# The last quarter of an MLP by two seven-product units, the final norm's factors by pieces, a tile pool 32 bytes lower, and relu squares on ScalarE

## The chip, the cores and the metric

The kernel runs on one core of a Trainium2 chip. Its engines are TensorE (PE, with PEld for its weight loads), VectorE (DVE), ScalarE (ACT), GpSimd (POOL) and SyncE (SP), which issues most DMAs. Each engine works through its own instructions in order and waits on semaphores for the others. The metric is the device time of one execution in microseconds (us), as the median of the runs.

## The reference

One layer of a streaming encoder for 256 tokens of width 2048 and 256 memory tokens, all float32:

```python
h = rms_norm(x, norm_mix_g);  x = x + hybrid_mixer(h, ...)      # retention + gated delta rule
h = rms_norm(x, norm_x_g);    x = x + cross_attention(h, rms_norm(mem, norm_mem_g), w_xq, w_xkv, w_xo)
h = rms_norm(x, norm_ffn_g);  x = x + square(relu(h @ w_ff1)) @ w_ff2   # 2048 -> 8192 -> 2048
return rms_norm(x, norm_final_g)        # x * rsqrt(mean(x*x) + 1e-6) * g
```

Here `x` is 256 by 2048, `w_ff1` 2048 by 8192, `w_ff2` 8192 by 2048. The change touches the MLP, the final norm, and where the tiles for memory lie.

## The kernel before

Every large product keeps float32 precision by three matmuls on a faster type: each operand is split into a high part (a ScalarE copy, L125) and a low part (a VectorE subtraction, L126), and high·high, high·low and low·high are added up in PSUM. Activations lie in quads: tiles of four feature blocks of 128, high and low beside each other (`q` in the trace). Weights come by DMA in pieces of 1 MB into `raw` (three buffers), and `fetch` converts each piece in two halves of 128x1024 into `whi` and `wlo` (three buffers, and every fourth pair `whx`, `wlx` in the MLP). `fetch` runs with a priority far ahead of other work, so that DMAs and conversions run ahead as far as the buffers go.

The stages, by the span of the profiled execution: cross-attention's values of the memory tokens (to 97 us: L401 to L403 and, in `chunk`, L166 to L168, with memory's quads as the stationary operand), its keys (to 191 us: `blocks`, L210 and L211, with memory's quads as the moving operand of a 512 and a 256 column matmul), the mixer (to 1066 us), output projection and cross-attention (to 1372 us), and the MLP.

The MLP runs in four quarters (`fb`) of 2048 hidden units, which start at 1372, 1527, 1697 and 1867 us. Each quarter first makes its hidden units with `blocks(h3, w_ff1, ...)`, eight times two blocks of 128 (L210 and L211), evacuated in `evac_h`: `bo` is the sum of two parts of PSUM (L220, L221), `hs` its squared relu, and hs is split into the quarter's quads. Then `with_seven` multiplies them by the quarter's rows of `w_ff2`, for four groups of 512 columns (n) and two halves of the tokens (t), by four quarters of the rows (q). A plain product (`plain(n, q)`) is 24 matmuls of 512 columns. A unit of seven products does what eight would (Strassen's way, Winograd's form) for the row quarters 0 and 1 and a pair of column groups: sums of token halves (`token_sums`, tile `sv`, its split `sh`, `sl`) times sums of weight blocks (b11, b12, b22, b21, made in place in the tiles `rt` and `tr`). One product (`product`) is 12 matmuls; it first converts its block in two halves (L1205, L1206) and, where `then` is given, makes a weight sum (L1210). `read` puts finished PSUM results on a list, and the next product's `read_now` adds them to the residual `res` on VectorE (`add`, L1141), behind the conversions that are out by then. All matmuls of plain and seven-product work have L1185. On PE the order is the order in which the code issues them (`ends` keeps the blocks and the products in turn).

The quarters 1 and 2 (`early`) have two such units for 16, so 14 products and 8 plain ones. The quarters 0 and 3 have one unit and twelve plain ones. In quarter 3 the last group of 512 columns is done by `chunk` at the very end, with its token half 1 in two halves of 256 columns, 96 half-width matmuls, and `evac_last` adds, squares, and scales. The final norm's sums of squares of the first three groups are taken on ScalarE (`square_sum`), their products with the final gain on VectorE (L1365), the root on POOL (L267); then each row block of 128 tokens is scaled by its root and written out. The final gains are read into `gfin`, which is the buffer of b22.

The tile pools lie behind one another in SBUF. PAD1 sets the length of a padding tile in front of the pool that holds memory's quads: these start at 117760 bytes of a partition and 4096 bytes on (multiples of 64). The activation quads (from 68064 on), weight tiles and the quads at 130016 and on start 32 bytes beside a multiple of 64.

Of the kernel before, what the change touches and what calls it, by code (L numbers as in the profile page):

```python
# [10 lines left out]
F32 = mybir.dt.float32  # L11
# [6 lines left out]
P = 128  # L18
D = 2048
# [15 lines left out]
PAD1, PAD2 = 144, 80  # L35
# [17 lines left out]
def trunk(ctx: ExitStack, tc: tile.TileContext, x_f, mem_f, positions, lead_f, small_f, w_in, ret_gn_g, w_out, w_xq,  # L53
# [1081 lines left out]
    gfin = b22  # L1135
# [8 lines left out]
    def add_later(n, t, ps):  # L1144

        with tc.issue_after(latest["lo"]):
            add(n, t, ps)

# [10 lines left out]
    def with_seven(hid, rows, last, early):  # L1159
# [39 lines left out]
        def product(o, lhs, raw, key, then=None):  # L1199

            halves = []
# [10 lines left out]
            for i in range(4):  # L1212
                ins = triple(o, lhs(i), [a[:, i % 2, :] for a in halves[i // 2]], key, i == 3)
            ends.append(ins)
# [11 lines left out]
        if early:  # L1226
# [20 lines left out]
            load_block(b12, 0, 3)  # L1247
            product(own[1][0], summed(3), b22, (1, 0))
# [3 lines left out]
            read((0, 0, own[0][0]))  # L1252
            product(own[0][1], part(1, 1), b11, (0, 1))
            read((0, 1, own[0][1]))
# [9 lines left out]
            read(*((1, t, own[1][t]) for t in range(NT)))  # L1264
# [9 lines left out]
            read(*((3, t, own[3][t]) for t in range(NT)))  # L1274
            product(own[2][0], part(1, 0), b21, (2, 0))
            read((2, 0, own[2][0]))
            product(shared, summed(2), b12, "shared")
            read((2, 1, shared), (3, 1, shared))
            product(own[2][1], part(1, 1), b11, (2, 1))
            read((2, 1, own[2][1]))  # L1280
        else:
# [3 lines left out]
            first = 2 if last else 3  # L1285
            plain(first, 0)
            load_block(b11, 0, 0)
            plain(first, 1)
# [3 lines left out]
            plain(first, 2)  # L1292
# [5 lines left out]
            plain(first, 3)  # L1298
            load_block(b21, 1, 0)
            read(*((first, t, own[first][t]) for t in range(NT)))  # L1300
# [5 lines left out]
            if not last:  # L1306
                plain(2, 0)
# [3 lines left out]
            if not last:  # L1311
                plain(2, 1)
            product(own[0][1], part(1, 1), b11, (0, 1))
            read((0, 1, own[0][1]))
            if not last:
                plain(2, 2)
                plain(2, 3)
                read(*((2, t, own[2][t]) for t in range(NT)))
            plain(1, 3)
            read(*((1, t, own[1][t]) for t in range(NT)))  # L1320
        for those in reads:
            add(*those)

    ends = []
    for fb in range(4):
        hid = []
        rows = w_ff2[0, fb * D:(fb + 1) * D, :]
        early = fb in (1, 2)
        parts_of = with_seven(hid, rows, fb == 3, early)
        ends.clear()  # L1330
        for b2 in range(8):
# [4 lines left out]
            def evac_h(b, ps):  # L1336
                if early and b2 > 3:
                    act.activation(ps, ps, AF.Relu)
                    act.activation(hs[:, b, :], ps, AF.Square)
                else:  # L1340
                    vec.scalar_tensor_tensor(hs[:, b, :], ps, 0.0, ps, op0=ALU.max, op1=ALU.mult)
# [13 lines left out]
        if fb < 3:  # L1355
            continue
        with tc.issue_after(fetched[-1]):
            nc.sync.dma_start(gfin, norm_final_g.partition_broadcast(P))
        for t in range(NT):
            for n in range(3):  # L1360
                ns = slice(n * 512, (n + 1) * 512)
                got = res[:, t, ns]
                square_sum(ssq4[:, t, n:n + 1], got)
                with tc.issue_after(latest["add"]):
                    vec.tensor_mul(got, got, gfin[:, ns])  # L1365
        for n in range(3, 4):
            ns = slice(n * 512, (n + 1) * 512)

            def evac_last(t, ps, c0, c1):
                got = add(n, t, ps, c0, c1)  # L1370
                acc = ssq4[:, t, 4 if c0 else 3:5 if c0 else 4]
                if t == 0:
                    square_sum(acc, got)
                else:
                    junk = sm.tile([P, 512], F32, name="junk", tag="junk", bufs=1)
                    vec.scalar_tensor_tensor(junk[:, :256], got, 1.0, got, op0=ALU.mult, op1=ALU.mult, accum_out=acc)
                if not c0:
                    s = sm.tile([P, 1], F32, name="s4", tag="s4")
                    vec.tensor_reduce(s, ssq4[:, t, 0:4], axis=AX.X, op=ALU.add)
                    vec.tensor_scalar(s, s, 1.0 / D, EPS, op0=ALU.mult, op1=ALU.add)  # L1380
                    sums.append(s)
                else:
                    vec.scalar_tensor_tensor(sums[t], acc, 1.0 / D, sums[t], op0=ALU.mult, op1=ALU.add)
                if c1 < 512:
                    return
                r = sm.tile([P, 1], F32, name="r4", tag="r4")
                rsqrt(r, sums[t])
                if t == 0:
                    vec.tensor_mul(res[:, t, ns], res[:, t, ns], gfin[:, ns])
                for c in (0, 3, 1, 2):  # L1390
                    cs = slice(c * 512, (c + 1) * 512)
                    o = res[:, t, cs]
                    if t and c == 3:
                        vec.scalar_tensor_tensor(o, o, r, gfin[:, cs], op0=ALU.mult, op1=ALU.mult)
                    elif t and c == 2:
                        vec.tensor_scalar(o, o, r, None, op0=ALU.mult)
                    else:
                        act.activation(o, o, AF.Copy, scale=r)
                    (act if t and c in (3, 2) else nc.sync).dma_start(out[0, t * P:(t + 1) * P, cs], o)

            sums = []
# [43 lines left out]
```

## Time and profile before

| | |
|---|---|
| median of 3 runs | 2051.8 us (2050.77 to 2052.64) |
| profiled execution | 2050.97 us, span 2049.2 us |
| granted clock of TensorE | 0.999 |
| PE, DVE, ACT, POOL busy | 99%, 75%, 56%, 2% |
| DMA | 405.24 MB, mean 198 GB/s |
| last quarter of the MLP | from 1867 us: blocks to 1956, second matrix to 2041, then norm and output |

The profile's span begins with the first instruction that it shows, and the execution has 1.77 us more around it. In the views a row is an instruction (start, length, engine, line, operation, output and inputs by tile) or a group of them. PE's ends are modelled, so its pace is read from one start to the next.

### The profile page before, as it was taken

How to read it: one execution, taken by the hardware profiler on the slowest of the kernel's cores; microseconds unless marked ns; L12 is line 12 of the kernel's file. 1: busy time of each engine (PE TensorE's matmuls, PEld its weight loads, DVE VectorE, ACT ScalarE, POOL GpSimd, SP SyncE). 2: the span in 40 equal slices, each digit the busy share in tenths (PEclk: the TensorE clock that was granted, in tenths of full speed). 3: DMA queues.
4: the chain of work that ended last, by engine and by line, in shares of the span. 5: the costliest groups of instructions: out<-in, count | busy, mean ns of one | idle time of the engine just before them, and what ended most of it. 6: DMA issues, size and time to landing. Idle time of an engine off the chain costs nothing.

```text
span 2049.2 us, 28493 instructions
## 1 busy us (share of the span) xinstructions
PE 2038.1 (99%) x10850; PEld 1756.6 (86%) x10850; DVE 1542.9 (75%) x2433; ACT 1153.2 (56%) x1871; POOL 36.3 (2%) x50
## 2 busy tenths in 40 slices
PE   9999999999999999999999999999999999999998
PEld 8888888988888888888888899888888888888887
DVE  5887788779667875888557666777868887888785
ACT  6655764575457555755446555555545655655554
POOL 0000000000000000000000000000000000000000
PEclk9999999999999999999999999999999999999999
DMA  9679556555555555555467655569657647555662
GB/s 327 204 253 301 185 183 196 164 185 195 187 168 181 194 196 165 184 182 189 156 206 248 191 180 163 173 180 257 219 169 234 219 159 218 200 199 159 220 217 103
DMA packets 329225, 405.24 MB, mean 198 GB/s; under 512 B 34928, under 2 KB 239360, under 8 KB 328960
## 3 DMA queue, kind: packets, MB, share of 16 engines
q1 hardware_dynamic: 328656, 402.74, 61.1%
q8 instruction: 85, 1.39, 0.3%
q10 hardware_dynamic: 432, 0.69, 0.1%
q14 instruction: 52, 0.43, 0.1%
HBM read 389.74 MB, written 11.55 MB: 196 GB/s over the span
## 4 chain that ended last, share of the span: by engine, by line
PE 96%; DMA 1%; DVE 1%; issue 1%; ACT 1%; SPq 0%; POOLq 0%; POOL 0%; DVEq 0%; ACTq 0%
PE s L210 33%; PE s L211 17%; PE s L167 8%; PE s L168 8%; PE s L166 8%; PE b L1185 7%; PE s L1185 6%; PE s L401 1%; PE s L403 1%; PE s L402 1%; PE b L796 1%; PE b L829 1%; PE b L138 0%; DMA raw<-w_ff 0%; PE b L137 0%
## 5 line engine op out<-in xcount | busy, mean ns | idle before, releaser
L210 PE MATMUL s<-q,whi 128*128 128x512 f32 x2816 | 972.6, 391 | 0.8 <-DVE bo L221 0.6
L126 DVE TENSOR_TENSOR wlo<-raw,whi 128x1024 fp32r<-128x1024 f32 x592 | 722.6, 1222 | 294.9 <-ACT whi L125 288.5
L125 ACT ACTIVATE whi<-raw 128x1024 fp32r<-128x1024 f32 x592 | 627.4, 1060 | 518.9 <-PE s L210 189.2
L211 PE MATMUL s<-q,wlo 128*128 128x256 f32 x2816 | 769.3, 280 | 0.7 <-DVE wlo L126 0.6
L210 PEld LDWEIGHTS s<-q,whi 128*128 128x128 f32 x2816 | 520.8, 188 | 102.9 <-DVE bo L221 0.9
L211 PEld LDWEIGHTS s<-q,wlo 128*128 128x128 f32 x2816 | 528.6, 188 | 13.1 <-DVE wlo L126 1.6
L167 PE MATMUL s<-wlo,q 128*128 128x512 f32 x716 | 281.6, 393 | 0.0
L168 PE MATMUL s<-whi,q 128*128 128x512 f32 x716 | 279.3, 390 | 0.0
L166 PE MATMUL s<-whi,q 128*128 128x512 f32 x716 | 258.9, 390 | 0.0
L166 PEld LDWEIGHTS s<-whi,q 128*128 128x128 f32 x716 | 134.3, 188 | 27.9
L168 PEld LDWEIGHTS s<-whi,q 128*128 128x128 f32 x716 | 134.6, 188 | 26.9
L167 PEld LDWEIGHTS s<-wlo,q 128*128 128x128 f32 x716 | 134.6, 188 | 26.7
L220 ACT ACTIVATE bo<-s 128x256 f32<-128x256 f32 x192 | 72.8, 379 | 107.2 <-PE s L211 107.1
L221 DVE TENSOR_TENSOR bo<-bo,s 128x256 f32<-128x256 f32 x192 | 79.9, 416 | 48.6 <-ACT bo L220 48.3
L125 ACT ACTIVATE whx<-raw 128x1024 fp32r<-128x1024 f32 x56 | 59.3, 1059 | 53.7 <-PE s L210 21.9
L210 PE MATMUL s<-q,whx 128*128 128x512 f32 x256 | 89.2, 389 | 0.0
L126 DVE TENSOR_TENSOR wlx<-raw,whx 128x1024 fp32r<-128x1024 f32 x56 | 68.4, 1221 | 24.6 <-ACT whx L125 24.1
L1185 PE MATMUL s<-whi,q 128*128 128x512 f32 x264 | 85.2, 389 | 0.0
L1185 PE MATMUL b<-whi,q 128*128 128x512 f32 x244 | 78.8, 389 | 0.0
L1206 DVE TENSOR_TENSOR wlo<-rt,whi 128x1024 fp32r<-128x1024 f32 x46 | 56.1, 1223 | 23.3 <-ACT whi L1205 22.5
L211 PE MATMUL s<-q,wlx 128*128 128x256 f32 x256 | 70.5, 280 | 0.0
L1205 ACT ACTIVATE whi<-rt 128x1024 fp32r<-128x1024 f32 x46 | 48.8, 1060 | 33.4 <-PE s L1185 15.3
(385 smaller groups left out, 2344.7 us busy)
## 6 DMA issues: line engine op xcount, KB each, us to landing
raw<-w_in SPq DMA_DIRECT2D x143, 1024.0 KB
raw<-w_ff SPq DMA_DIRECT2D x104, 1024.0 KB
raw<-w_xkv SPq DMA_DIRECT2D x29, 1024.0 KB
raw<-w_out SPq DMA_DIRECT2D x16, 1024.0 KB
raw<-w_xq SPq DMA_DIRECT2D x16, 1024.0 KB
raw<-w_xo SPq DMA_DIRECT2D x16, 1024.0 KB
rt<-w_ff SPq DMA_DIRECT2D x12, 1024.0 KB
tr<-w_ff SPq DMA_DIRECT2D x12, 1024.0 KB
```

Of the source, the lines that this page charges most:

```text
L125: latest["hi"] = act.activation(hi[:, cs], src[:, cs], AF.Copy).ins
L126: latest["lo"] = vec.tensor_sub(lo[:, cs], src[:, cs], hi[:, cs].bitcast(F32)).ins
L166: pe.matmul(o, xh, wh, start=first, stop=False)
L167: pe.matmul(o, xh, wl, start=False, stop=False)
L168: pe.matmul(o, xl, wh, start=False, stop=last)
L210: pe.matmul(ps[b], lh, xhl, start=kk == 0, stop=False)
L211: ins = pe.matmul(ps[b][:, :S], ll, xh, start=False, stop=kk == KT - 1).ins
L220: act.activation(o, ps[b][:, S:], AF.Copy)
L221: vec.tensor_add(o, o, ps[b][:, :S])
L1185: ins = pe.matmul(o, lhs[l], rhs[r], start=key not in opened, stop=last and j == 2, skip_group_check=True).ins
L1205: latest["hi"] = act.activation(hi, raw[:, c:c + 1024], AF.Copy).ins
L1206: latest["lo"] = vec.tensor_sub(lo, raw[:, c:c + 1024], hi.bitcast(F32)).ins
```

## The change

The change has four parts.

1. `PAD1` goes from 144 to 136 floats: all tiles of the pool behind it, memory's quads among them, start 32 bytes lower (117728).
2. `early` holds for quarter 3 too: it has 14 products and 8 plain ones. Its last product goes in two halves of 256 columns into two PSUM tiles, 24 half-width matmuls.
3. The final norm's factors come by pieces: as soon as a piece of `res` is complete, `settle` takes its squares on ScalarE and multiplies it by the final gain on VectorE, in the middle of the products. The gains have a quad buffer of their own and are fetched in the middle of the quarter. Row block 0's root and scaling are issued ahead of the last product's sums; row block 1's last piece is squared on VectorE, in two halves.
4. In the quarters 1 to 3 all of `evac_h`'s squared relus run on ScalarE (Relu in PSUM, then Square into `hs`); before, ScalarE had those of the last four of eight steps in the quarters 1 and 2, and VectorE had the others.

```diff
-PAD1, PAD2 = 144, 80
+PAD1, PAD2 = 136, 80
...
+    def settle(n, t):
+        got = res[:, t, n * 512:(n + 1) * 512]
+        square_sum(ssq4[:, t, (0, 1, 3, 2)[n]:(1, 2, 4, 3)[n]], got)
+        vec.tensor_mul(got, got, final[0][:, n * 512:(n + 1) * 512])
+
+    def mean_square(t):
+        s = sm.tile([P, 1], F32, name="s4", tag="s4")
+        vec.tensor_reduce(s, ssq4[:, t, 0:4], axis=AX.X, op=ALU.add)
+        vec.tensor_scalar(s, s, 1.0 / D, EPS, op0=ALU.mult, op1=ALU.add)
+        sums.append(s)
+
+    def finish_row(t):
+        r = sm.tile([P, 1], F32, name="r4", tag="r4")
+        rsqrt(r, sums[t])
+        for c in (0, 2, 1, 3):
+            cs = slice(c * 512, (c + 1) * 512)
+            o = res[:, t, cs]
+            if t and c == 2:
+                vec.scalar_tensor_tensor(o, o, r, final[0][:, cs], op0=ALU.mult, op1=ALU.mult)
+            elif t and c == 3:
+                vec.tensor_scalar(o, o, r, None, op0=ALU.mult)
+            else:
+                act.activation(o, o, AF.Copy, scale=r)
+            (act if t and c > 1 else nc.sync).dma_start(out[0, t * P:(t + 1) * P, cs], o)
...
         def read_now():
-            for those in reads:
-                add_later(*those)
+            for n, t, ps, *done in reads:
+                add_later(n, t, ps)
+                if last and done:
+                    settle(n, t)
...
             load_block(b12, 0, 3)
+            if last:
+                final.append(quad_a().both.rearrange("p k s -> p (k s)").bitcast(F32))
+                with tc.issue_after(fetched[-1]):
+                    nc.sync.dma_start(final[0], norm_final_g.partition_broadcast(P))
...
-            read((0, 0, own[0][0]))
+            read((0, 0, own[0][0], True))
...
             product(own[2][0], part(1, 0), b21, (2, 0))
-            read((2, 0, own[2][0]))
+            read((2, 0, own[2][0], True))
+            if last:
+                read((2, 1, own[2][1]))
             product(shared, summed(2), b12, "shared")
-            read((2, 1, shared), (3, 1, shared))
-            product(own[2][1], part(1, 1), b11, (2, 1))
-            read((2, 1, own[2][1]))
+            if last:
+                mean_square(0)
+                finish_row(0)
+            read((2, 1, shared), (3, 1, shared, True))
+            if not last:
+                product(own[2][1], part(1, 1), b11, (2, 1))
+                read((2, 1, own[2][1]))
+            else:
+                ends_of = stream_ps()
+                product(ends_of, part(1, 1), b11, "end")
+                for c, ps in enumerate(ends_of):
+                    got = add(2, 1, ps[:, :256], c * 256, c * 256 + 256)
+                    junk = sm.tile([P, 512], F32, name="junk", tag="junk", bufs=1)
+                    acc = ssq4[:, 1, 3 + c:4 + c]
+                    vec.scalar_tensor_tensor(junk[:, :256], got, 1.0, got, op0=ALU.mult, op1=ALU.mult, accum_out=acc)
+                    if c:
+                        vec.scalar_tensor_tensor(sums[1], acc, 1.0 / D, sums[1], op0=ALU.mult, op1=ALU.add)
+                    else:
+                        mean_square(1)
+                finish_row(1)
...
-        early = fb in (1, 2)
+        early = fb > 0
...
-                if early and b2 > 3:
+                if early:
                     act.activation(ps, ps, AF.Relu)
                     act.activation(hs[:, b, :], ps, AF.Square)
...
-            chunk(hid, cols(rows, n * 512), evac_last, hold=quad_b)
```

The instructions of all engines stand in the same order up to the MLP's quarter 1, where the squared relus move; PE's and the DMA queue's up to quarter 3.

First place: VectorE at the very end of the program. In the names, `res` is the residual, `s0`, `s1` and `b` are PSUM tiles, `junk` receives squares whose sum goes to `ssq4`, `tr` and (after) `q` hold the final gains, and L1153 is the new product by the gain. Before:

```order
L1141 SCALAR_TENSOR_TENSOR res_13006<-s0_18616,rstd3q_13000,res_13006 128x512
L1379 TENSOR_REDUCE s4_18754<-ssq4_13012 128x1
L1389 TENSOR_TENSOR res_13006<-res_13006,tr_13007 128x512
L1380 TENSOR_SCALAR s4_18754<-s4_18754 128x1
L1141 SCALAR_TENSOR_TENSOR res_13006<-s1_18617,rstd3q_13000,res_13006 128x256
L1376 SCALAR_TENSOR_TENSOR junk_18793,ssq4_13012<-res_13006 128x256
L1379 TENSOR_REDUCE s4_18795<-ssq4_13012 128x1
L1380 TENSOR_SCALAR s4_18795<-s4_18795 128x1
L1141 SCALAR_TENSOR_TENSOR res_13006<-b_18618,rstd3q_13000,res_13006 128x256
L1376 SCALAR_TENSOR_TENSOR junk_18823,ssq4_13012<-res_13006 128x256
L1383 SCALAR_TENSOR_TENSOR s4_18795<-ssq4_13012,s4_18795 128x1
```

And now, behind the last product's last conversion:

```order
L1153 TENSOR_TENSOR res_13006<-res_13006,q_18324 128x512
L1157 TENSOR_REDUCE s4_18789<-ssq4_13012 128x1
L1141 SCALAR_TENSOR_TENSOR res_13006<-b_17779,rstd3q_13000,res_13006 128x512 x2
L1158 TENSOR_SCALAR s4_18789<-s4_18789 128x1
L1141 SCALAR_TENSOR_TENSOR res_13006<-s0_18802,rstd3q_13000,res_13006 128x256
L1141 SCALAR_TENSOR_TENSOR res_13006<-s1_18803,rstd3q_13000,res_13006 128x256
L1153 TENSOR_TENSOR res_13006<-res_13006,q_18324 128x512
L1329 SCALAR_TENSOR_TENSOR junk_18842,ssq4_13012<-res_13006 128x256
L1157 TENSOR_REDUCE s4_18844<-ssq4_13012 128x1
L1329 SCALAR_TENSOR_TENSOR junk_18848,ssq4_13012<-res_13006 128x256
L1158 TENSOR_SCALAR s4_18844<-s4_18844 128x1
L1331 SCALAR_TENSOR_TENSOR s4_18844<-ssq4_13012,s4_18844 128x1
```

Before, the first half's square and sum stood ahead of the last add; now the product by the gain, both squares and the sum stand behind it.

Second place: VectorE in the middle of the last quarter's products, at the plain product of column group 3 and row quarter 2, whose conversions are the L126 of `raw_18648` (L1239 makes weight sums). Now:

```order
L126 TENSOR_TENSOR wlx_18595<-raw_18588,whx_18594 128x1024
L1235 TENSOR_TENSOR wlo_18627<-tr_13007,whi_18626 128x1024
L1141 SCALAR_TENSOR_TENSOR res_13006<-b_17780,rstd3q_13000,res_13006 128x512 x2
L1153 TENSOR_TENSOR res_13006<-res_13006,q_18324 128x512
L1235 TENSOR_TENSOR wlo_18631<-tr_13007,whi_18630 128x1024
L1239 TENSOR_TENSOR rt_10152<-tr_13007,rt_10152 128x1024 x2
L1153 TENSOR_TENSOR res_13006<-res_13006,q_18324 128x512
L126 TENSOR_TENSOR wlo_18651<-raw_18648,whi_18650 128x1024
L126 TENSOR_TENSOR wlx_18655<-raw_18648,whx_18654 128x1024
```

Before, the products by the gain stood behind the last of the products, among the last chunk's conversions:

```order
L126 TENSOR_TENSOR wlo_18684<-raw_18681,whi_18683 128x1024
L1141 SCALAR_TENSOR_TENSOR res_13006<-s0_18157,rstd3q_13000,res_13006 128x512
L1141 SCALAR_TENSOR_TENSOR res_13006<-s1_18158,rstd3q_13000,res_13006 128x512
L1365 TENSOR_TENSOR res_13006<-res_13006,tr_13007 128x512
L126 TENSOR_TENSOR wlx_18688<-raw_18681,whx_18687 128x1024
L1365 TENSOR_TENSOR res_13006<-res_13006,tr_13007 128x512 x5
```

Six products by the gain stood in one place with a single conversion behind the first; now they lie one by one among the conversions.

More of the change, by code (lines that the diff above doesn't have):

```diff
@@ L1263, in with_seven @@
             plain(1, 3)
-            read(*((1, t, own[1][t]) for t in range(NT)))
+            read(*((1, t, own[1][t], True) for t in range(NT)))
             product(p5, summed(0), b11, "p5", (b11, b22, b11))
@@ L1310, in with_seven @@
             read((0, 1, shared), (1, 1, shared))
-            if not last:
-                plain(2, 1)
+            plain(2, 1)
             product(own[0][1], part(1, 1), b11, (0, 1))
             read((0, 1, own[0][1]))
[L1315 to L1318, printed above, removed]
+            plain(2, 2)
+            plain(2, 3)
+            read(*((2, t, own[2][t]) for t in range(NT)))
             plain(1, 3)
             read(*((1, t, own[1][t]) for t in range(NT)))
-        for those in reads:
-            add(*those)
+        for n, t, ps, *_ in reads:
+            add(n, t, ps)
     ends = []
@@ L1354, in trunk @@
             pass
[L1355 to L1401, printed above, removed]
-            chunk(hid, cols(rows, n * 512), evac_last, hold=quad_b)
```

28 lines of the change are left out of this document (14 added, 14 removed).

## The prediction

> **What bounds the kernel now.** I read the page's busy shares first, then its chain of work that ended last:
>
> ```profile
> PE 2038.1 (99%) x10850; PEld 1756.6 (86%) x10850; DVE 1542.9 (75%) x2433; ACT 1153.2 (56%) x1871; POOL 36.3 (2%) x50
> PE 96%; DMA 1%; DVE 1%; issue 1%; ACT 1%; SPq 0%; POOLq 0%; POOL 0%; DVEq 0%; ACTq 0%
> ```
>
> TensorE (PE) is busy for 99% of the span and is 96% of the chain. So time goes only where there are fewer matmuls, where one takes less, where PE stops waiting, or in the tail behind the last matmul. The profiled execution took 2050.97 us, 0.83 below the median of 2051.8. I sum against 2050.97 and add 0.83 at the end. A measurement of this kernel can tell about 0.2% from no change, 4.1 us: faster means under 2047.7, slower over 2055.9.
>
> **Memory's quads, 32 bytes lower.** PE's timeline shows the pace of 512-column matmuls while those quads are the stationary operand (L401 to L403 and L167), and the chain a stretch of the MLP where the pace is that of other operands:
>
> ```profile
> 21.15 0.40 PE L401 MATMUL s<-whi,q 128*128 128x512 f32 x1
> ...
> 49.62 0.40 PE L403 MATMUL s<-whi,q 128*128 128x512 f32 x1
> ...
> 76.16 0.40 PE L167 MATMUL s<-wlo,q 128*128 128x512 f32 x1
> ...
> 90.16 0.40 PE L167 MATMUL s<-wlo,q 128*128 128x512 f32 x1
> 1626.30 24.48 PE s L1185 x108
> ```
>
> From the first to the second are 122 matmuls: 28.47 / 122 = 233.4 ns. From the third to the fourth are 60: 14.00 / 60 = 233.3 ns. In the MLP 24.48 / 108 = 226.7 ns. Is it DMA traffic? The views by windows (length, then busy us of PE, PEld, DVE, ACT, POOL, then granted clock, DMA share, GB/s) speak against it:
>
> ```profile
> 10.00:65.00 55.00, 55.00 (x237) 44.29 (x236) 35.58 (x44) 33.53 (x46) 0.00 (x0) 1.00 0.90 319
> 76.00:93.00 17.00, 17.00 (x75) 13.68 (x74) 16.91 (x29) 9.94 (x13) 0.00 (x0) 1.00 0.47 143
> 1815.00:1820.00 5.00, 5.00 (x24) 4.14 (x23) 4.15 (x5) 2.35 (x3) 0.00 (x0) 1.00 1.02 360
> ```
>
> The slow pace is the same at 319 and at 143 GB/s, at a full clock; at 360 GB/s an MLP stretch starts 22 to 24 matmuls in 5 us, no fewer than 226.7 ns allows. What only the slow stretches share is the operand. Memory's quads start at multiples of 64 bytes; every other weight or activation tile of the large products lies 32 bytes beside one, and the change puts memory's there too. The values have 378 such matmuls: 378 × 6.6 ns = 2.5 us. In the keys the quads are the moving operand of a 512 and a 256 column matmul in turn:
>
> ```profile
> 145.00:190.00 45.00, 44.30 (x130) 23.46 (x130) 1.00 0.97 320
> 1380.00:1440.00 60.00, 59.93 (x175) 32.56 (x175) 1.00 1.03 264
> ```
>
> These windows count L210 alone, one a pair: with one pair more or less at an edge (45 / 129 and 60 / 174), 348.8 ns a pair in the keys, 344.8 in the MLP. 256 pairs × 4.0 ns = 1.0 us. I take **−3.5**, with 0 and −3.6 as ends.
>
> A page of the Trainium skill speaks against this term. "SBUF — State Buffer", section "Who interferes with whom", gives PE two independent read ports, one for the moving operand and one for weight loads, shared with nobody, and nothing in it makes a start address cost time. By it this term would be 0. The rows above bear out that the slow pace isn't traffic; no run here shows yet that it is the address. It is a rival below.
>
> **One product fewer in the last quarter.** The quarter's ff2 now has two units of seven products for one unit and three plain products, and the half-width form of the last 512 columns goes from 96 matmuls to 24. PE's timeline has the half-width ones:
>
> ```profile
> 2038.12 0.28 PE L166 MATMUL s<-q 128*128 128x256 f32 x1
> ...
> 2041.24 0.28 PE L168 MATMUL b<-q 128*128 128x256 f32 x1
> ```
>
> 26 steps in 3.12 us are 120 ns each. Before: 324 × 226.7 + 96 × 120 ns = 84.97 us. After: 348 × 226.7 + 24 × 120 ns = 81.77. That is **−3.2**, arithmetic on counts.
>
> **Stalls that go with the old end.** The trace shows PE starting late five times where plain chunk and products met in the old order:
>
> ```profile
> 2010.82 0.61 PE L1185 MATMUL s<-whi,q 128*128 128x512 f32 x2
> 2011.68 0.50 PE L1185 MATMUL s<-wlo,q 128*128 128x512 f32 x1 [0.25 <-DVE wlo L1206]
> 2012.02 0.62 PE L1185 MATMUL s<-whi,q 128*128 128x512 f32 x2
> ...
> 2013.62 0.28 PE L166 MATMUL b<-whi,q 128*128 128x256 f32 x1
> 2014.13 0.50 PE L1185 MATMUL s<-wlo,q 128*128 128x512 f32 x1 [0.23 <-DVE wlo L126]
> 2014.47 0.40 PE L1185 MATMUL s<-whi,q 128*128 128x512 f32 x1
> ```
>
> From 2010.82 two starts should take 0.45 us and take 0.86 (0.41 lost), the next one 0.34 for 0.23 (0.11), from 2013.62 0.51 for 0.12 (0.39), then 0.34 for 0.23 (0.11): **−1.0**. That order is gone. What is late next is the following part.
>
> **New work on VectorE (DVE).** The section that the last quarter now copies is the third quarter's, 1796 to 1867.6:
>
> ```profile
> 1796.00:1867.60 71.60, 71.60 (x317) 59.24 (x317) 61.70 (x62) 40.10 (x42) 0.00 (x0) 1.00 0.49 162
> 2020.52 0.68 DVE L1365 TENSOR_TENSOR res<-res,tr 128x512 f32<-128x512 f32 x1
> 2021.12 1.22 DVE L126 TENSOR_TENSOR wlx<-raw,whx 128x1024 fp32r<-128x1024 f32 x1
> ```
>
> DVE is busy 61.70 of 71.60 us there. The change adds seven products by the final gain, each 0.60 us from its start to the next one's: 4.2 us, so some 66 of 70.8, or 94%. PE waits for a conversion only where the work ahead of it on DVE piles up. I find two such places.
>
> ```profile
> 1838.83 1.40 DVE L1141 SCALAR_TENSOR_TENSOR res<-b,rstd3q,res 128x512 f32<-128x512 f32 x2
> 1840.15 1.22 DVE L1206 TENSOR_TENSOR wlo<-tr,whi 128x1024 fp32r<-128x1024 f32 x1
> ...
> 1843.55 1.22 DVE L126 TENSOR_TENSOR wlo<-raw,whi 128x1024 fp32r<-128x1024 f32 x1
> 1844.69 1.22 DVE L126 TENSOR_TENSOR wlx<-raw,whx 128x1024 fp32r<-128x1024 f32 x1
> 1845.69 0.39 PE L1185 MATMUL s<-wlo,q 128*128 128x512 f32 x1
> ...
> 1860.14 1.23 DVE L1206 TENSOR_TENSOR wlx<-rt,whx 128x1024 fp32r<-128x1024 f32 x1 [0.18 <-ACT whx L1205]
> 1864.28 0.39 PE L1185 MATMUL b<-whi,q 128*128 128x512 f32 x1
> ```
>
> First, the plain product of columns 3, row quarter 2: two gain products now stand ahead of its conversions (second order fence), 1.20 us. In the third quarter that conversion ended at 1844.77 and PE used it at 1845.69, 0.92 us later. 1.20 − 0.92 gives a wait of 0.3. Second, the last product: from 1860.14 DVE has, ahead of the last conversion's end, a conversion, an add, a gain product, an add and two conversions, 1.14 + 0.66 + 0.60 + 0.66 + 1.14 + 1.22 = 5.42 us (0.66 an add where adds follow each other). That ends 1.28 us after the last product's start at 1864.28, and the half-width form uses the converted piece's low part after 7 of its matmuls, 7 × 0.12 = 0.84: a wait of 0.45. Together **+0.8**; 0 and 2 are the ends, since a gain product also waits for a square on ScalarE, which the trace of before doesn't have here.
>
> **The tail.**
>
> ```profile
> 2039.20 0.43 DVE L1376 SCALAR_TENSOR_TENSOR junk<-res 128x256 f32<-128x256 f32 x1
> 2039.67 0.16 DVE L1379 TENSOR_REDUCE s<-ssq 128x1 f32<-128x4 f32 x1
> ...
> 2041.56 0.48 DVE L1141 SCALAR_TENSOR_TENSOR res<-b,rstd3q,res 128x256 f32<-128x256 f32 x1 [1.54 <-PE b L168]
> 2042.08 0.42 DVE L1376 SCALAR_TENSOR_TENSOR junk<-res 128x256 f32<-128x256 f32 x1
> 2042.55 0.16 DVE L1383 SCALAR_TENSOR_TENSOR s<-ssq,s 128x1 f32<-128x1 f32 x1
> 2042.78 0.55 POOL L267 TENSOR_TENSOR r<-s,nhalf_pow 128x1 f32<-128x1 f32 x1 [3.92 <-DVE s L1383]
> ```
>
> Before, one add, one square and one small sum stand between PE's end E (2041.24 + 0.12 = 2041.36) and the root on POOL at 2042.78: 1.42 us. Now (first order fence) DVE reaches the last add late, since after the last conversion (E − 2.05) it has a gain product, two adds and two small operations and the first half's add, some 2.5 us: E + 0.44. Behind the last add (0.40) come a gain product (0.60), the first half's square (0.47), its sum (0.10), the second square (0.47), two small operations (0.10 and 0.19) and the hop (0.23): POOL starts at E + 3.0. I take **+1.5**, with 0.8 and 2 as ends (the lower if DVE isn't late and small ones hide). Row 0 is scaled on ScalarE meanwhile, and its output leaves earlier.
>
> **Relu on ScalarE.** 32 evacuations leave DVE in the quarters 1 to 3 and become 64 instructions on ScalarE:
>
> ```profile
> L1341 DVE SCALAR_TENSOR_TENSOR hs<-bo x48: 416/421/427, 1373.3 to 1958.3; 128x256 f32<-128x256 f32 x48
> L1339 ACT ACTIVATE hs<-bo x16: 398/401/403, 1585.9 to 1798.1; 128x256 f32<-128x256 f32 x16
> 1867.60:1912.00 44.40, 44.40 (x260) 39.36 (x259) 33.32 (x54) 23.00 (x33) 0.00 (x0) 1.00 0.68 206
> ```
>
> DVE loses 32 × 0.421 = 13.5 us, ScalarE gains 64 × 0.40 = 25.6, and in a window of block work it is busy 23.00 of 44.40 us, so 16 more (6.4 us) find room: **0** on the path. If that cover weren't there, a pair in front of a conversion would cost PE up to 0.4 us.
>
> **Sum.** −3.5 − 3.2 − 1.0 + 0.8 + 1.5 = −5.4: 2045.6 in the profiled form, and 0.83 more for the median, **2046.4**. Its own range, with the terms' ends mixed, is 2045 to 2048.
>
> **The rivals.** *The address does nothing*, and the slow pace of the first 191 us has another cause: 2046.4 + 3.5 = 2049.9, within 0.2%. For it is that only one stage shows the pace; against it, that the pace ends with the last use of those quads, whatever the traffic. Chance 0.22. *No new stall and a tail no longer than before*: 2046.4 − 0.8 − 1.5 = 2044.1; for it, that DVE has been rid of 13.5 us; against it, the rows of the order. Chance 0.08. *VectorE becomes the bound*, the slower side: each gain product waits for its square on ScalarE, which can stand behind conversions there, and DVE waits in order with the conversions for PE behind it. The page's group of ScalarE's conversions prices it:
>
> ```profile
> L125 ACT ACTIVATE whi<-raw 128x1024 fp32r<-128x1024 f32 x592 | 627.4, 1060 | 518.9 <-PE s L210 189.2
> ```
>
> With three of 1.06 us ahead of the square a wait is 3.2 us, seven are 22.3; DVE has 71.6 − 61.7 − 4.2 = 5.7 us of room, so PE would lose 16.6: about 2063. It decides for slower from 9.5 us more than forecast, that is from five of the seven waiting in full (5 × 3.2 = 16, less 5.7). Against it: in DVE's order most gain products stand behind further adds and conversions, which gives the square its time. Chance 0.05. *ScalarE's relu holds PE up* 16 times by 0.40 us: 2052.8. Chance 0.03; 23.00 of 44.40 us speaks against it. The Trainium skill, "ScalarE: Activation LUTs", section "Rules for kernel authors", sends relu and mul to VectorE; here the trace has 2 × 401 ns against 421, so the rule holds for the work, but not for the engine that has room.
>
> **How the numbers follow.** The forecast has 0.62. The range takes in it, the case without the address and the case without new costs: 2044.0 to 2050.2; the two dearer rivals are left out (0.08), and what of the three lies beyond its edges. Faster by over 0.2% is most of the forecast and the cheapest case, less what of the forecast's upper end passes 2047.7: 0.62. Within 0.2% are the address rival, that upper end and the relu rival: 0.33. Slower: 0.05.
>
> **What would show it.** Right: the pace of L401 to L403 at 227 ns from the first chunk on, and the keys' end 3.5 us earlier; 348 full and 24 half-width matmuls in the last ff2 section, with waits of 0.3 and 0.5 us at columns 3 and the last product; POOL's last root 3.0 us after PE's end. Wrong: an unchanged 233 ns, or DVE waiting for ScalarE ahead of gain products with PE idle behind it.

## The result, and the profile after

The changed kernel takes 2046.88 us (median of 8 runs, 2045.48 to 2048.38) against 2052.02 before (8 runs, 2050.77 to 2053.05): a ratio of 0.9975, interval 0.9965 to 0.9986. The forecast was 2046.4 in a range of 2044.0 to 2050.2. The profiled execution has a span of 2045.2 us for 2049.2.

Busy shares and the chain, from the page of the changed kernel:

```profile
PE 2033.4 (99%) x10802; PEld 1751.9 (86%) x10802; DVE 1550.1 (76%) x2422; ACT 1185.1 (58%) x1941; POOL 39.8 (2%) x50
PE 98%; DVE 1%; DMA 0%; ACT 0%; issue 0%; SPq 0%; POOLq 0%; POOL 0%; ACTq 0%
```

TensorE has 48 matmuls fewer and is still 99% busy. The values of memory, on PE's timeline:

```profile
20.99 0.39 PE L401 MATMUL s<-whi,q 128*128 128x512 f32 x1
...
48.87 0.39 PE L401 MATMUL s<-whi,q 128*128 128x512 f32 x1
```

123 matmuls in 27.88 us: 226.7 ns, where the kernel before had 233.4. PE's timeline at the two places of the last quarter for which a wait was forecast:

```profile
2013.07 0.61 PE L1213 MATMUL s<-whi,q 128*128 128x512 f32 x2
2013.86 0.50 PE L1213 MATMUL s<-wlo,q 128*128 128x512 f32 x1 [0.17 <-DVE wlo L126]
2014.19 0.40 PE L1213 MATMUL s<-whi,q 128*128 128x512 f32 x1
...
2032.58 0.28 PE L1213 MATMUL s<-whi,q 128*128 128x256 f32 x1
2032.76 0.39 PE L1213 MATMUL s<-wlo,q 128*128 128x256 f32 x1
2032.99 0.40 PE L1213 MATMUL s<-whi,q 128*128 128x256 f32 x2
...
2033.34 0.40 PE L1213 MATMUL s<-whi,q 128*128 128x256 f32 x2
2033.90 0.39 PE L1213 MATMUL s<-wlo,q 128*128 128x256 f32 x1 [0.16 <-DVE wlo L1235]
2034.12 0.40 PE L1213 MATMUL s<-whi,q 128*128 128x256 f32 x2
```

Both are there. At columns 3 the starts from 2013.07 on lose 0.34 and 0.10 us against 226.7 ns a matmul; in the last product those from 2032.58 on lose 0.06, 0.11, 0.32 and 0.10 against 120 ns: 0.44 and 0.59 us. VectorE's timeline shows what the last product waited for:

```profile
2031.50 2.35 DVE L1235 TENSOR_TENSOR wlo<-rt,whi 128x1024 fp32r<-128x1024 f32 x2
```

The second of these two conversions ends at 2033.85, 1.27 us after the last product's first matmul at 2032.58 (1.28 was forecast), and TensorE uses its result at 2033.90, after seven matmuls. That wait costs 0.42 of the 0.59 us; the other 0.17 lie at the first two half-width starts, which the forecast had at no cost.

Then the tail, from the timelines of VectorE, POOL and ScalarE; PE ends at 2036.03 (its last start 2035.91 + 0.12):

```profile
2034.37 0.15 DVE L1157 TENSOR_REDUCE s<-ssq 128x1 f32<-128x4 f32 x1
2034.43 1.40 DVE L1141 SCALAR_TENSOR_TENSOR res<-b,rstd3q,res 128x512 f32<-128x512 f32 x2
2035.75 0.14 DVE L1158 TENSOR_SCALAR s<-s 128x1 f32<-128x1 f32 x1
...
2035.97 0.55 POOL L267 TENSOR_TENSOR r<-s,nhalf_pow 128x1 f32<-128x1 f32 x1 [673.90 <-DVE s L1158]
2036.55 3.95 ACT L1172 ACTIVATE res<-res,r 128x512 f32<-128x512 f32 x6
...
2038.59 0.56 POOL L267 TENSOR_TENSOR r<-s,nhalf_pow 128x1 f32<-128x1 f32 x1 [2.07 <-DVE s L1331]
```

Row block 0's sum is ready at 2034.4, but its last small operation (L1158) stands behind two adds, so its root starts only at 2035.97; row block 1's starts 2.56 us after PE's end. The end of the span lies 9.17 us behind PE's end, where it lay 7.84 behind. The windows of the tail (last two columns: DMA share and GB/s) tell what fills it:

```profile
2036.00:2038.00 2.00, 0.19 (x2) 0.00 (x0) 1.97 (x7) 2.00 (x5) 0.52 (x1) 1.00 0.00 0
2038.00:2040.00 2.00, 0.00 (x0) 0.00 (x0) 1.30 (x6) 1.94 (x4) 0.56 (x1) 0.93 0.95 349
2040.00:2042.00 2.00, 0.00 (x0) 0.00 (x0) 0.32 (x1) 0.51 (x1) 0.00 (x0) 0.50 1.03 378
2042.00:2044.00 2.00, 0.00 (x0) 0.00 (x0) 0.00 (x0) 0.00 (x0) 0.00 (x0) 0.50 0.87 322
```

From 2038 on the outputs run without a gap at about 380 GB/s until nearly 2044: both row blocks, 2 MB. In the kernel before row block 0's root started at 2038.31, 3.05 us ahead of PE's end, and its output was over before row block 1's began:

```profile
2038.31 0.55 POOL L267 TENSOR_TENSOR r<-s,nhalf_pow 128x1 f32<-128x1 f32 x1 [674.01 <-DVE s L1380]
```

```profile
2040.00:2042.00 2.00, 1.52 (x13) 1.32 (x11) 0.46 (x2) 1.46 (x3) 0.00 (x0) 1.00 0.77 285
2042.00:2044.00 2.00, 0.00 (x0) 0.00 (x0) 1.26 (x5) 0.63 (x1) 0.55 (x1) 1.00 0.64 240
2044.00:2046.00 2.00, 0.00 (x0) 0.00 (x0) 0.52 (x2) 0.71 (x2) 0.00 (x0) 0.77 0.54 199
2044.00:2045.00 1.00, 0.00 (x0) 0.00 (x0) 0.52 (x2) 0.71 (x2) 0.00 (x0) 1.00 0.04 14
```

One place moved that nobody had touched, the output projection's blocks at 1065 to 1157 us. L210's matmuls there, in the same window of before and of after:

```profile
1090.00:1145.00 55.00, 54.62 (x160) 29.50 (x160) 1.00 0.72 222
```

```profile
1090.00:1145.00 55.00, 54.66 (x157) 28.94 (x156) 1.00 0.66 203
```

Fewer pairs in the same time: from start to start a 512-column matmul took 226.9 ns before and 235.8 now, and the kernel lost 0.8 us on its lead. The span's 4.0 us are: 2.9 gained up to 1065 us, 0.8 lost in the output projection, 0.1 gained up to 1865, 3.0 gained in the last quarter (173.9 us of PE's time to 170.8), 1.3 lost in the tail.

### The profile page after: what moved, and what is told of

The parts are those of the page before. It is cut to its first block, busy times and chain, and to the rows that moved or that the text cites. A ratio compares the mean times of both kernels' runs of the same rounds, so it can differ in the third digit from the quotient of the medians.

```text
span 2045.2 us, 28450 instructions
## 1 busy us (share of the span) xinstructions
PE 2033.4 (99%) x10802; PEld 1751.9 (86%) x10802; DVE 1550.1 (76%) x2422; ACT 1185.1 (58%) x1941; POOL 39.8 (2%) x50
## 4 chain that ended last, share of the span: by engine, by line
PE 98%; DVE 1%; DMA 0%; ACT 0%; issue 0%; SPq 0%; POOLq 0%; POOL 0%; ACTq 0%
PE s L210 34%; PE s L211 18%; PE s L167 8%; PE s L168 8%; PE s L166 8%; PE s L1213 7%; PE b L1213 7%; PE s L403 1%; PE s L401 1%; PE s L402 1%; PE b L796 1%; PE b L699 1%; PE b L829 1%; PE b L138 0%; PE b L137 0%; PE b L139 0%
## 5 line engine op out<-in xcount | busy, mean ns | idle before, releaser
L210 PE MATMUL s<-q,whi 128*128 128x512 f32 x2816 | 973.3, 391 | 0.8 <-DVE bo L221 0.6
L126 DVE TENSOR_TENSOR wlo<-raw,whi 128x1024 fp32r<-128x1024 f32 x584 | 712.7, 1221 | 298.5 <-ACT whi L125 294.1
L125 ACT ACTIVATE whi<-raw 128x1024 fp32r<-128x1024 f32 x584 | 618.8, 1060 | 499.3 <-PE s L210 208.8
L210 PEld LDWEIGHTS s<-q,whi 128*128 128x128 f32 x2816 | 520.7, 188 | 103.4 <-DVE bo L221 0.9
L167 PE MATMUL s<-wlo,q 128*128 128x512 f32 x704 | 277.2, 394 | 0.0
L168 PE MATMUL s<-whi,q 128*128 128x512 f32 x704 | 274.9, 391 | 0.0
L166 PE MATMUL s<-whi,q 128*128 128x512 f32 x704 | 254.4, 391 | 0.0
L166 PEld LDWEIGHTS s<-whi,q 128*128 128x128 f32 x704 | 132.1, 188 | 27.3
L168 PEld LDWEIGHTS s<-whi,q 128*128 128x128 f32 x704 | 132.3, 188 | 26.2
L1235 DVE TENSOR_TENSOR wlo<-rt,whi 128x1024 fp32r<-128x1024 f32 x56 | 68.2, 1223 | 32.8 <-ACT whi L1234 32.0
L210 PE MATMUL s<-q,whx 128*128 128x512 f32 x256 | 89.1, 389 | 0.0
L1213 PE MATMUL s<-whi,q 128*128 128x512 f32 (+1 forms) x280 | 88.8, 383 | 0.0
L126 DVE TENSOR_TENSOR wlx<-raw,whx 128x1024 fp32r<-128x1024 f32 x60 | 73.3, 1221 | 19.0 <-ACT whx L125 18.8
L1234 ACT ACTIVATE whi<-rt 128x1024 fp32r<-128x1024 f32 x56 | 59.3, 1060 | 39.6 <-PE s L1213 19.2
L1213 PE MATMUL b<-whi,q 128*128 128x512 f32 x220 | 71.5, 389 | 0.0
```

The costliest lines, as they stand in the source:

```text
L125: latest["hi"] = act.activation(hi[:, cs], src[:, cs], AF.Copy).ins
L126: latest["lo"] = vec.tensor_sub(lo[:, cs], src[:, cs], hi[:, cs].bitcast(F32)).ins
L166: pe.matmul(o, xh, wh, start=first, stop=False)
L167: pe.matmul(o, xh, wl, start=False, stop=False)
L168: pe.matmul(o, xl, wh, start=False, stop=last)
L210: pe.matmul(ps[b], lh, xhl, start=kk == 0, stop=False)
```

## The experiments

All ratios are to the kernel before, by runs on the same chip. Times, where three or more runs were made, are medians.

**The address alone (b_low, a_high).**

```diff
-PAD1, PAD2 = 144, 80
+PAD1, PAD2 = 136, 80
```

> The kernel before with PAD1 = 136 alone: memory's quads 32 bytes lower, nothing else. Theory (the start address sets the pace): the values' 512-column matmuls go from 233.3 to 226.7 ns, the keys' pairs lose some 3 to 4 ns, the keys' end comes 2.9 us earlier, and the time is 2.9 us lower, about 2049.1 (ratio 0.9986). Rival (the address does nothing, the faster start in the changed kernel is of another cause): 233.3 ns again and 2052.0. Second question: in the changed kernel the blocks from 1065 to 1157 us ran all at 236 ns a 512-column matmul, where the kernel before ran at 227 from 1085 on. If that comes with the address too, it shows here, and takes 0.8 us back (2049.9).

Measured: 2048.54 against 2051.68, ratio 0.9984 (0.9975 to 0.9993). The values on PE's timeline of this kernel:

```profile
20.87 0.39 PE L401 MATMUL s<-whi,q 128*128 128x512 f32 x1
...
48.75 0.39 PE L401 MATMUL s<-whi,q 128*128 128x512 f32 x1
```

Again 123 in 27.88 us, 226.7 ns. The order of the instructions is the one of before and only the tiles of that pool lie elsewhere, so the address is the cause, and the rival falls. Against the kernel before, this one is 2.3 us ahead at the end of the values and 2.95 at the end of the keys. The other way round, the changed kernel with PAD1 = 144:

> The changed kernel with PAD1 = 144 again: memory's quads back at multiples of 64 bytes. Theory: 233.3 ns again in the values, and 2.2 to 2.9 us slower than the changed kernel, 2049.1 to 2049.8 (ratio to the kernel before 0.9986). Rival (the address does nothing): 2046.9. The blocks from 1065 to 1157 us run at 227 ns from 1085 on if their pace goes with this address, at 236 if not.

Measured: 2049.76, ratio 0.9989 (0.9980 to 0.9997), 2.9 us above the changed kernel's median; 233.3 ns in the values. In both kernels the output projection ran at 227 ns from 1085 us on, so its pace doesn't go with this address.

**Relu alone (b_relu).** In the kernel before:

```diff
-                if early and b2 > 3:
+                if fb > 0:
```

> The kernel before with all squared relus of the quarters 1 to 3 on ScalarE, nothing else. Theory (hidden): the same time as before within 0.5 us, and no new wait of TensorE in the MLP's blocks. Rival (ScalarE holds TensorE up, 0.40 us each time): up to 6.4 us slower, about 2058.

Measured: 2051.76 against 2051.68, ratio 1.0 (0.9992 to 1.0009). The move to ScalarE costs nothing that can be measured.

**The last product by the gain behind the last sum (a_late_mul).** In the changed kernel, `settle` leaves out the product of the last piece, and at the end:

```diff
+                with tc.issue_after(summed_up):
+                    vec.tensor_mul(res[:, 1, 1536:2048], res[:, 1, 1536:2048], final[0][:, 1536:2048])
                 finish_row(1)
```

> The changed kernel with the last product by the final gain (columns 3 of row block 1) put behind the last sum of squares, into VectorE's wait for the root. Theory (the tail is the queue on VectorE): the root on POOL starts 2.0 us after TensorE's end for 2.56, and the time is 0.6 us lower, 2046.3. Rival (the tail is set by ScalarE's six scalings or by the outputs' DMAs): the root comes earlier and the end of the span stays within 0.2 us.

Measured: 2046.64, ratio 0.9974 (0.9964 to 0.9985), and a span of 2045.3, as the changed kernel's 2045.2. VectorE and POOL on the timeline:

```profile
2037.80 0.69 DVE L1336 TENSOR_TENSOR res<-res,q 128x512 f32<-128x512 f32 x1
2037.96 0.94 POOL L267 TENSOR_TENSOR r<-s,nhalf_pow 128x1 f32<-128x1 f32 x1 [1.46 <-DVE s L1332]
2038.93 0.75 DVE L1169 SCALAR_TENSOR_TENSOR res<-res,r,q 128x512 f32<-128x512 f32 x1 [0.45 <-POOL r L267]
```

Row block 1's root starts 0.63 us earlier (2037.96 for 2038.59), and the end stays: the rival held, the tail isn't set by that root. Beside the product on VectorE the root took 0.94 us for 0.55, so most of the lead was gone at its end anyhow.

**Two products by the gain behind a conversion (a_shift_mul).** `settle` puts column group 1 on a list, and:

```diff
             plain(3, 2)
+            with tc.issue_after(latest["lo"]):
+                for got in due:
+                    vec.tensor_mul(got, got, final[0][:, 512:1024])
```

> The changed kernel with the two products by the gain of column group 1 put behind the conversions of the plain product of column group 3, row quarter 2. Theory (these two products ahead of the conversion make TensorE wait there): the wait of 0.45 us at 2013.3 is gone, and the time is 0.4 us lower. Rival (the weight sums and the other conversion ahead of it are enough for a wait): 0.2 us or more of it stays.

Measured: the wait at columns 3 is gone, and the last quarter's PE time falls from 170.84 to 170.36 us. But the time is 2047.91 (ratio 0.9984, 0.9974 to 0.9993). The new order put another add and a product by the gain ahead of row block 0's last small operation, and POOL's timeline shows its root:

```profile
2037.01 0.55 POOL L267 TENSOR_TENSOR r<-s,nhalf_pow 128x1 f32<-128x1 f32 x1 [674.72 <-DVE s L1161]
2038.54 0.56 POOL L267 TENSOR_TENSOR r<-s,nhalf_pow 128x1 f32<-128x1 f32 x1 [0.98 <-DVE s L1337]
```

Row block 0's root is 1.04 us later than in the changed kernel, row block 1's 0.05 earlier, and the end of the span lies 10.3 us behind PE's end for 9.17. With a_late_mul this settles it: row block 0's root, and 2 MB of outputs behind it, set the end.

**Another order in the tail (a_tail).** With the products of column group 1 moved as above:

```diff
+            if key == "end":
+                with tc.high_priority(offset=60000), tc.issue_after(latest["lo"]):
+                    latest["lo"] = mean_square(0)
             read_now()
...
-            if t and c == 2:
+            if t and c > 1:
                 vec.scalar_tensor_tensor(o, o, r, final[0][:, cs], op0=ALU.mult, op1=ALU.mult)
-            elif t and c == 3:
-                vec.tensor_scalar(o, o, r, None, op0=ALU.mult)
```

> The changed kernel with the two products by the gain of column group 1 behind the conversions of the plain product of columns 3, row quarter 2, and a tail in another order: row block 0's sum and root straight behind the last conversion, its product by the gain after them; row block 1's last two pieces scaled and multiplied by the gain in one instruction each; its square on ScalarE between row block 0's scalings. Theory (the tail is the start of row block 0's outputs, and 2 MB of outputs behind it at 380 GB/s): row block 0's root starts 2 us earlier against TensorE's end than in the changed kernel, the end of the span comes 0.5 to 1 us earlier, and the wait at columns 3 is gone too: 2045.5 to 2046. Rival (row block 1's root sets the end): it comes only 0.3 us earlier, and so does the end.

Measured: 2046.20, ratio 0.9970 (0.9958 to 0.9982), the lowest median of all, 0.7 below the changed kernel's, which these runs can't tell apart from it. POOL's timeline and the windows of the tail:

```profile
2034.23 0.93 POOL L267 TENSOR_TENSOR r<-s,nhalf_pow 128x1 f32<-128x1 f32 x1 [672.28 <-DVE s L1167]
2038.48 0.56 POOL L267 TENSOR_TENSOR r<-s,nhalf_pow 128x1 f32<-128x1 f32 x1 [3.32 <-DVE s L1344]
```

```profile
2036.00:2038.00 2.00, 0.24 (x3) 0.04 (x1) 1.65 (x7) 2.00 (x5) 0.00 (x0) 1.00 0.61 228
2038.00:2040.00 2.00, 0.00 (x0) 0.00 (x0) 1.30 (x6) 1.30 (x3) 0.56 (x1) 0.71 0.79 293
2040.00:2042.00 2.00, 0.00 (x0) 0.00 (x0) 0.48 (x1) 0.40 (x1) 0.00 (x0) 0.50 0.70 259
```

Row block 0's root comes 1.74 us earlier, the outputs start before 2038 but run with gaps now, and the end lies 8.8 us behind PE's: 0.35 gained, not 0.5 to 1. With row block 0 early, row block 1's root is late next, as the rival said. The wait at columns 3 is gone here too.

**A wait put in on purpose (a_wait, a_wait64, a_all).** In the output projection, ahead of the third pair of blocks, with `z` a small tile of the pool in front of memory's quads:

```diff
+                    with tc.issue_after(order[-1]):
+                        first = pe.matmul(bank()[:, :2], ident, z, start=True, stop=True).ins
+                    with tc.high_priority(offset=100000):
+                        rsqrt(z, half_pow[:, :2])
+                    with tc.issue_after(first):
+                        order.append(pe.matmul(bank()[:, :2], ident, z, start=True, stop=True).ins)
```

> The changed kernel with one wait put in on purpose: between the first two and the third pair of blocks of the output projection (about 1073 us) TensorE multiplies a 2-column tile, waits until POOL has rewritten it, and multiplies it again. Six profiles so far show two paces in these blocks with the same instructions at the same addresses: 226.7 ns a 512-column matmul in the three where TensorE had to wait 0.15 to 1.0 us for a late conversion near 1080 us (the stage takes 90.7 to 91.6 us), 235.4 ns in the three where it hadn't (92.4 us). Theory (a wait makes TensorE fall into the faster rhythm): 226.7 ns from the wait on, the stage takes 91.4 us with a wait of 0.7, and the time is 0.5 to 1 us lower than the changed kernel's slower profiles. Rival (the pace is set by something else that also makes the conversion late, such as the timing of the DMAs): 235.4 ns goes on behind the wait, and the stage takes 93 us.

Measured: 2057.83, ratio 1.0032 (1.0019 to 1.0044). The waits of TensorE, and L210's matmuls in the window used above:

```profile
PE b L1041 <- POOL n_z L267: 0.8, 1, 0.8
```

```profile
1090.00:1145.00 55.00, 54.65 (x161) 29.54 (x160) 1.00 0.69 214
```

The pace is the fast one, 161 pairs for 157. But PE's timeline shows that it didn't need the wait that was put in:

```profile
1068.78 0.50 PE L210 MATMUL s<-q,whi 128*128 128x512 f32 x1 [0.22 <-DVE q L134]
...
1069.94 0.39 PE L210 MATMUL s<-q,whi 128*128 128x512 f32 x1
...
1071.31 0.39 PE L210 MATMUL s<-q,whi 128*128 128x512 f32 x1
...
1072.77 0.38 PE L1041 MATMUL b<-n_z,ident 128*128 128x2 f32 x2 [0.83 <-POOL n_z L267]
```

At 1068.78 TensorE waited 0.22 us for a split activation, which it does in none of the kernels without this edit, and the four pairs from 1069.94 to 1071.31 took 1.37 us, for 1.41 in the changed kernel: the fast pace was there before the put-in wait at 1072.77. It is the same in a_wait64 and a_all. So the theory isn't tested by these runs as it was meant to be.

The time went elsewhere: the tile took 32 bytes, so all tiles behind it moved, memory's quads back to 117760, the MLP's input quads from 130016 to 130048 bytes, and whx and wlx too. The values ran at 233.3 ns. By the starts of the same matmuls, a_wait lies 3.1 us behind the changed kernel at the end of the keys, 2.6 at the end of the mixer, 2.7 behind the output projection with the wait in it, 3.5 at the start of the MLP and 11.5 near its end. So the wait didn't cost the 10 us: 8 of them came in the MLP, where 512-column matmuls took 230.8 ns on average for 227.0.

> The changed kernel with the one wait of the kernel a_wait, its 2-column tile now in 64 bytes instead of 8 (which the pool made 32): the tiles behind it move by 64 bytes and stay 32 beside a multiple of 64. Theory (in a_wait it was the 32 bytes that took 10 us: memory's quads and, at 130048 bytes and on, the quads of the MLP's and the attention's inputs came to lie on multiples of 64): 226.7 ns in the values again, 226.7 to 227.2 ns in the output projection from the wait on with the stage at 91.3 us, and a time 0.5 to 1.1 us below the changed kernel's, about 2046. Rival (the wait itself, or the changed order of the DMAs around it, took the 10 us): 2057 again.

Measured: 2063.32, ratio 1.0055 (1.0043 to 1.0068), with 233.3 ns in the values at 117792 bytes, which is 32 beside a multiple of 64. That theory fell: 32 beside a multiple of 64 isn't enough. The MLP's 512-column matmuls took 230.4 ns on average. The last run combines a_tail and the wait, with 128 bytes for the tile:

> The kernel a_tail with the one wait of a_wait, its small tile now in 128 bytes, so that every tile behind it keeps its start address modulo 128. Seven kernels put memory's quads at 0, 16, 32, 64, 96 and 112 modulo 128, and 96 alone, where all weight tiles lie too, ran at 226.7 ns. Theory (the address modulo 128 took the time of a_wait and a_wait64, and the wait switches the pace of the output projection): 226.7 ns in the values, 226.7 to 227.2 ns in the output projection from the wait at 1073 us on, the stage some 1 us shorter than a_tail's, the MLP at its old pace, and 2045.2 to 2045.7 us, the fastest of all. Rival (the wait or the changed order of DMAs around it took the time): 2057 or more. Rival for the pace alone: 235.4 ns behind the wait, and 2047.

Measured: 2061.54, ratio 1.0045 (1.0031 to 1.0059). The output projection again ran fast behind the wait (160 pairs in the window), but the values ran at 233.3 ns, and the MLP's 512-column matmuls took 231.0 ns on average. So a place modulo 128 isn't the rule either.

**Other start addresses (a_pad128, a_pad140, a_pad148).** The changed kernel with PAD1 = 128, 140 and 148.

> The changed kernel with PAD1 = 128: memory's quads start at 117696 bytes, a multiple of 64 again but not of 1024 as at 117760 (115 x 1024). Theory (a multiple of 64 is what costs): 233.3 ns in the values. Rival (what costs is the place within a larger block, or the distance to the weight tiles): 226.7 ns.

> The changed kernel with PAD1 = 140: memory's quads start at 117744 bytes, 48 beside a multiple of 64. Theory (only multiples of 64 cost): 226.7 ns in the values. Rival (only 32 beside a multiple of 64 is free): 233.3 ns, or more.

> The changed kernel with PAD1 = 148: memory's quads start at 117776 bytes, 16 beside a multiple of 64. At 0 and 48 beside it the values ran at 233.3 ns, at 32 at 226.7. Theory (only 32 beside a multiple of 64 is free): 233.3 ns. Rival (16 and 32 are free): 226.7 ns.

Measured, one run each: 2049.68, 2049.63 and 2051.65 us, with 233.3 ns in the values of all three. PE's timeline of a_pad148:

```profile
21.37 0.39 PE L401 MATMUL s<-whi,q 128*128 128x512 f32 x1
...
49.37 0.39 PE L401 MATMUL s<-whi,q 128*128 128x512 f32 x1
```

120 in 28.00 us. Two of these edits don't do what their expectations say. The pool gives a tile a multiple of 32 bytes (as it made 32 of a_wait's 8), so a padding of 140 floats (560 bytes) takes 576, as 144 floats do, and one of 148 (592 bytes) takes 608. In the built programs memory's quads start at 117760 in a_pad140, which is instruction for instruction the program of a_high, and at 117792 in a_pad148, the start of a_wait64. No run put them at 117744 or 117776, 48 or 16 beside a multiple of 64. So the expectation of a_all counts two places that weren't run, 16 and 112 modulo 128. Five starts were:

| start, bytes | kernels | modulo 64, 128, 256 | ns a matmul in the values |
|---|---|---|---|
| 117696 | a_pad128 | 0, 64, 192 | 233.3 |
| 117728 | changed, b_low, a_late_mul, a_shift_mul, a_tail | 32, 96, 224 | 226.7 |
| 117760 | before, b_relu, a_high, a_pad140, a_wait | 0, 0, 0 | 233.3 |
| 117792 | a_pad148, a_wait64 | 32, 32, 32 | 233.3 |
| 117856 | a_all | 32, 96, 96 | 233.3 |

The one fast start is 224 beside a multiple of 256, and so are, in the changed kernel, the starts of all weight tiles (whi from 42720, wlo from 55776, whx, wlx) and of all other quads. In `blocks`, though, the high part of the weights begins 224 bytes into its tile (`AT_BLOCKS = (56, 0)`), so at 192 beside a multiple of 256, and the MLP's blocks ran at 226.8 ns.

## Why the prediction was right, point by point

- **The address.** −3.5 was forecast and 2.9 to 3.1 measured (2.96 in the profile by the end of the keys, 3.1 in b_low's median, 2.9 between a_high and the changed kernel). The two parts of the term were both a little too large: in b_low the values gave 2.3 us for 2.5, the keys 0.6 for 1.0. That the slow pace belongs to the operand's place and not to traffic is shown. The wording, multiples of 64 against 32 beside one, doesn't hold: 117792 and 117856 are 32 beside one too and are slow, and in `blocks` the high part of the weights starts at a multiple of 64 (42944 in the first whi) and was fast already before. The rule of the Trainium skill's page "SBUF — State Buffer" ("Who interferes with whom"), by which the term would be 0, doesn't decide this: the pace changed by 3% with a start address alone.
- **One product fewer, and the old stalls.** With the new waits, −3.2 − 1.0 + 0.8 = −3.4 was forecast for PE's last quarter, and −3.03 measured. The count and the old stalls held; the new waits came at the two places named, at 0.44 and 0.59 us for 0.3 and 0.45. a_shift_mul shows the first one's cause: without the two products by the gain ahead of the conversion it is gone. For the second the queue on VectorE is the one forecast, instruction by instruction, but no run took it away, so its cause stays argued.
- **The tail.** +1.5 was forecast, +1.33 measured, but by another road. The forecast priced the queue ahead of row block 1's root (E + 3.0; it was E + 2.56) and let row block 0's output leave early. It left out the transfer: row block 0's root waited for a small operation behind two adds, and 2 MB of outputs then ran back to back. a_shift_mul shows it: with that root 1.04 us later the end came 1.1 us later behind PE's end. The size came out near by luck.
- **Relu.** 0 was forecast, and b_relu shows it.
- **What was not foreseen.** The output projection lost 0.8 us in the profile, by its second pace. With the address 0.6 short of its forecast and PE's last quarter 0.4, and the tail 0.2 better, it makes the profile's lead 4.0 us for the forecast 5.4. The medians lie 5.1 us apart.

## What to carry to other kernels

Where one stage of a matmul-bound kernel runs a few per cent slower at the same clock and under less traffic, try its operands' start addresses. Read them from the built program, not from the edit: here the pool rounded two of the paddings up to starts that had been run already. And remember that any small tile put ahead of the operands in a pool moves them all: with 32 to 128 bytes for a scratch tile the kernel was 11 to 16 us slower here, mostly in stages whose operands had moved. When all rows of an output are finished at the end, price their transfer too, since then the first row's root counts and the last one's does not. An edit that frees a wait on a busy engine reorders its queue elsewhere, so look at the end of that queue before counting the gain.

## What the runs showed of the hardware that was not expected

**A matmul's pace goes with the start address of its operand**, 226.7 or 233.3 ns for 512 columns with it as the stationary one. One of five starts was fast. No run moved whi and wlo, but a_wait64 moved whx and wlx by 64 bytes, as far as the MLP's input quads (to 32 beside a multiple of 256, both). With these quads as the moving operand, a 512-column matmul of its MLP's blocks took 226.8 ns with whx and 231.8 with the unmoved whi; in the changed kernel both took 226.8. So the pace there went with the places of the two operands to each other, and 224 beside a multiple of 256 isn't needed by itself. It isn't the whole rule: in a_wait and a_all, where whx had moved with the quads too, it took 229.4 and 229.6 ns. The rule stays open.

**The same instructions at the same addresses have two paces.** The output projection's moving quads (from 68064 bytes) and weight tiles lay at the same place in all kernels. In fourteen profiles TensorE, or its weight load, had a wait of 0.2 to 1.1 us between 1065 and 1095 us in six: the kernels before, b_low and a_high, and the three kernels with a wait put in, where another of 0.2 us came first. From 1090 to 1145 us a 512-column matmul took 226.7 to 227.1 ns in all six, and 235.4 to 235.8 in the eight without one. The clearest pair is a_high and a_pad140, which are the same program: with a wait at 1080 us 226.8 ns, without one 235.7, and 1.5 us of the 1.8 between their spans came in this stage. So neither the code nor the addresses alone set this pace. That a wait switches it is likely, since the pace turns within 2 us behind the first wait each time, but isn't shown: in the kernels where a wait was put in, the fast pace had begun before it. By what means a wait would do so is open. The spread of one kernel's runs (2.9 us for the changed kernel) may come from this, since a late conversion near 1080 us is a matter of the DMAs' timing.

**POOL's root is held up by VectorE.** 128x1 on POOL took 0.55 to 0.56 us in the changed kernel and 0.94 (a_late_mul) and 0.93 (a_tail) while VectorE multiplied two tiles of SBUF. The same page and section of the Trainium skill says that a VectorE instruction with two SBUF inputs contends with a GpSimd instruction that reads SBUF; the trace agrees.
